# Moving the tiles of a one-core hybrid attention / recurrence layer to 512-byte starts

## The chip, the cores and the metric

The kernel runs on one core of one Trainium2 chip. The metric is the device time of one execution in microseconds (us); lower is better. A profile of one execution is read beside the times. Five kinds of rows appear in it: PE is the matrix engine's matmul stream, PEld its weight loads, DVE the vector engine, ACT the scalar engine, POOL the GpSimd engine; SP only issues transfers.

## The reference

One layer of an encoder for 512 tokens of width 2048, everything in float32. An RMS norm and one projection to 4608 columns give q (8 heads of 128), k and v (2 heads), an attention gate, a recurrent branch's input and its gate. Cut to what matters:

```python
h = rms_norm(x, norm_w)
q, k, v, g_attn, xr, g_lru = split(h @ w_in)            # w_in (2048, 4608)
attn_out = softmax(rope(norm(q)) @ rope(norm(k)).T / sqrt(128)) @ v
xc  = depthwise_conv4(xr) + conv_b
lru = scan(a_fwd, b_fwd) + reversed_scan(a_bwd, b_bwd)  # gates: 128x128 blocks of xc
mixed = concat(rms_norm(attn_out) * silu(g_attn), rms_norm(lru) * silu(g_lru))
return x + mixed @ w_out                                # w_out (2048, 2048)
```

## The kernel before

Each float32 matrix is split into a high and a low part in the matrix engine's rounded float32 format (fp32r), and each product is three matmuls: high by high, high by low, low by high (`mm3`, lines 145 to 147). Nearly all matmuls have a 128 x 128 stationary operand (the one that a weight load brings in ahead of the matmul, 512 bytes of each partition) and a 128 x 512 moving operand (2,048 bytes of each partition, streamed past it). In `nc.tensor.matmul(acc, a, b)`, `a` is stationary and `b` moving.

The order of the matrix engine's work is written out by hand (`manual_schedule`), in these stages, with the times of the profile:

- 0 to 55 us: x is transposed block by block (`xturn`, line 230, 128-column float32 matmuls against the identity `ident`), woven into the first projection (`proj_feat`: weights stationary, x moving).
- 55 to 198 us: a second such projection and k/v (`proj_tok`: x stationary, weights moving) with the recurrence gates (`lru_pair`) between.
- 198 to 262 us: the two q projections (`proj_tok`). Here `wsplit` (lines 204, 205) puts every other pair of weight blocks in a second pool, `wx`.
- 262 to 430 us: attention in 32 steps, with the three gate projections (`proj_feat`) as filling work between. A step makes the scores of 128 queries (`weights`: q slices stationary, `kt` moving), turns an earlier step's probabilities (`turn_weights`, line 575, four 128-column matmuls: the probabilities stationary, `ident` moving), and every fourth step multiplies with v (`values`: v slices stationary, `pt` moving).
- 430 to 498 us: the last gate projection.
- 498 to 654 us: the output projection (`outputs`, line 891) by a scheme with 7 products in place of 8. There are 224 groups of three matmuls: a slice of a combination of the mixed activations is stationary (`mh`, `ml`, eight entries in `mixed`), a combination of `w_out` blocks is moving (`oh`, `ol`). The combination number n goes to slot n % 7 (`operand`): slots 0 to 2 lie in the pool `fin`, slots 3 to 6 in the pool `out`. Entries 0 to 4 of `mixed` lie in `fin` and in the ring `hring`, entries 5 to 7 in `out`.

On-chip memory is laid out by two stacks of pools in each partition. The left stack grows upward: constants (`cp`), raw weights (`wr`), x and split weights (`xw`, later `out`), `rope`, `rot`. The right stack grows downward from byte 229,376: a pad (`end`), the rings of the recurrence and attention results (`hq`), then one after another `lru`, `qkv` with `wx`, `att`, and `fin`. A tile of 4 bytes takes 32. These are the start bytes of tiles that matmuls read, from the program's allocations:

| tile | stack | start byte, example | start modulo 512 |
|---|---|---|---|
| x (`x2`), weights in `xw` (`wh`, `wl`) | left | 37,376; 20,992 | 0 |
| `mh`, `ml`, `oh`, `ol` in `out` | left | 25,088; 88,576 | 0 |
| `ident` | left | 1,152 | 128 |
| weights in `wx` | right | 147,328; 155,520 | 384 |
| raw x blocks, gate operands in `lru` | right | 130,944; 163,712 | 384 |
| `kt`, `v`, rotated q (`ev`) in `qkv` | right | 186,240; 161,664; 176,000 | 384 |
| probabilities turned (`pt`) in `att` | right | 145,280 | 384 |
| probabilities (`k2`) in `att` | right | 126,656 | 192 |
| split q (`b4`) in `att` | right | 110,080 | 0 |
| `mh`, `ml`, `oh`, `ol` in `fin`, `hring` | right | 110,464; 186,240; 196,480 | 384 |

Inside `att` the order from high to low bytes is `pt`, `sm`, `k2`, `mx`, `b4`. `mx` and `sm` hold one number for each query (the row maximum, and the sum of exponentials and its reciprocal), in 6 buffers each: 192 bytes each.

Of the kernel before, what the change touches and what calls it, by code (L numbers as in the profile page):

```python
# [10 lines left out]
F32 = mybir.dt.float32  # L11
# [5 lines left out]
P = 128  # L17
# [38 lines left out]
def hybrid_kernel(  # L56
# [25 lines left out]
    pools, order = {}, {"left": [], "right": []}  # L82

    def opened(name, side):
        pools[name] = tc.alloc_tile_pool(name=name, bufs=1, side=side, reuse_waits="tile")
        order[side].append(name)
        return pools[name]
# [8 lines left out]
    cp = opened("cp", "left")  # L96
    opened("wr", "left")
    opened("xw", "left")
    opened("end", "right").tile([P, 24], F32, tag="end", name="end")
    hring = opened("hq", "right").ring(8 * 2048, name="hring")  # L100
    aring = pools["hq"].ring(8 * 2048, name="aring")
    opened("lru", "right")
# [5 lines left out]
    def nm(s):  # L108
        cnt[0] += 1
        return f"{s}_{cnt[0]}"  # L110
# [7 lines left out]
    def k2(dt=F32, shape=(P, SEQ)):  # L118
        pool, n, _ = work()
        return pools[pool].tile(list(shape), dt, tag="k2", bufs=n, name=nm("k2"))  # L120
# [14 lines left out]
    def mm():  # L135
        return ps.tile([P, SEQ], F32, tag="mm", name=nm("mm"))
# [7 lines left out]
    def mm3(acc, lh, ll, rh, rl, start, stop):  # L144
        nc.tensor.matmul(acc, lh, rh, start=start, stop=False)  # L145
        nc.tensor.matmul(acc, lh, rl, start=False, stop=False)  # L146
        nc.tensor.matmul(acc, ll, rh, start=False, stop=stop)  # L147
# [408 lines left out]
    def weights(q, g, t):  # L556

        qh, ql = q
        tt = slice(t * P, (t + 1) * P)
        sc = mm()  # L560
        mm3(sc, qh[:, tt], ql[:, tt], kth[g], ktl[g], True, True)
        mx = pools["att"].tile([P, 1], F32, tag="mx", bufs=6, name=nm("mx"))
        nc.vector.tensor_reduce(mx, sc, axis=AX.X, op=ALU.max, negate=True)  # L563
        p = k2()
        sm = pools["att"].tile([P, 1], F32, tag="sm", bufs=6, name=nm("sm"))
        nc.scalar.activation(p, sc, AF.Exp, bias=mx, accum_out=sm)
        nc.vector.reciprocal(sm, sm)
        nc.gpsimd.tensor_scalar(p, p, sm, 0.0, op0=ALU.mult, op1=ALU.add)
        return p
# [27 lines left out]
    def attention(rots):  # L597

        qs, ps_, pts = {h: turned(rots[0], h) for h in range(2)}, {}, {}
        yield 13  # L600
        last = NH * NT
        for i in range(last + 3):
            h, t = divmod(i, NT)
            if i < last:
                ps_[i] = weights(qs[h], h // G, t)
                if t == 0 and h + 2 < NH:
                    qs[h + 2] = turned(rots[(h + 2) // G], (h + 2) % G)
            j = i - 3
            if j >= 0 and j % NT == NT - 1:
                values(j // NT, *pts.pop(j // NT))  # L610
            j = i - 2
            if 0 <= j < last:
                h, t = divmod(j, NT)
                if t == 0:
                    pts[h] = [
                        pools["att"].tile([P, NT, SEQ], F32R, tag="pt", bufs=ATT_PT, name=nm("pt"))
                        for _ in range(2)
                    ]
                turn_weights(ps_.pop(j), t, *pts[h])
            yield STEPS  # L620
# [522 lines left out]
```

## Time and profile before

| | |
|---|---|
| median of 3 runs | 661.3 us (661.18 to 662.85) |
| the profiled execution | 660.07 us, of it 658.3 us from the first to the last instruction |
| granted clock of the matrix engine | 0.998 |
| PE busy | 651.0 us, 2971 instructions |
| DVE, ACT, POOL busy | 488.2, 345.6, 92.1 us |
| transfers | 96.17 MB, mean 146 GB/s |

The busy time of PE hides how close its matmuls follow each other: matmuls overlap, and a row's duration (about 390 ns) is longer than the distance from one start to the next. So the distances of starts are what to read: the chain of waits gives, for a run of matmuls with one output bank kind, the start, the length from this start to the next run's, and the count.

### The profile page before, as it was taken

To read this page: it belongs to the slowest core of one execution; us is meant where nothing else is said; L and a number is where in the kernel's file an instruction comes from. 1 tells how busy PE (TensorE), PEld (TensorE's weight loads), DVE (VectorE), ACT (ScalarE), POOL (GpSimd) and SP (SyncE) were. 2 spreads that over 40 slices of the span, in tenths; PEclk is the share of its full clock that TensorE was granted. 3 is DMA by queue.
4 is the path that set the end of the run, shared out by engine and by line. 5 is a ranking of instruction groups with operands and counts; after the bars stand their busy time and mean duration, and the time that the engine had idled before them with its cause. 6 is when DMAs were issued, how large, how long until landed. Compare 5 with 4: busy or idle time off the path is not lost.

```text
span 658.3 us, 8625 instructions
## 1 busy us (share of the span) xinstructions
PE 651.0 (99%) x2971; PEld 534.1 (81%) x2971; DVE 488.2 (74%) x843; ACT 345.6 (53%) x639; POOL 92.1 (14%) x121
## 2 busy tenths in 40 slices
PE   8999999999999999999999999999999999999997
PEld 6888888888888888888888888888888888888875
DVE  5879688977687952855955568439958998698994
ACT  3533898489856515453744446435444564334441
POOL 0000000000022301233443335410000000000000
PEclk9999999999999999999999999999999999999999
DMA  8843252322334321346875768663355766585322
GB/s 291 288 131 93 65 167 65 97 64 67 93 121 135 92 69 32 102 143 154 179 186 138 192 141 199 158 140 95 96 177 199 259 210 237 189 293 181 132 77 96
DMA packets 52731, 96.17 MB, mean 146 GB/s; under 512 B 4184, under 2 KB 14544, under 8 KB 52560
## 3 DMA queue, kind: packets, MB, share of 16 engines
q1 hardware_dynamic: 45648, 75.17, 36.1%
q0 software_dynamic: 6720, 19.93, 13.1%
q10 hardware_dynamic: 320, 0.53, 0.3%
q8 instruction: 23, 0.38, 0.2%
q14 instruction: 20, 0.16, 0.1%
HBM read 91.42 MB, written 20.97 MB: 171 GB/s over the span
## 4 chain that ended last, share of the span: by engine, by line
PE 96%; DVE 1%; DMA 1%; issue 1%; ACT 0%; ACTq 0%; DVEq 0%
PE pj L145 20%; PE pj L147 20%; PE pj L146 20%; PE mm L891 12%; PE pj L891 9%; PE mm L145 3%; PE mm L147 3%; PE mm L146 3%; PE mm L575 2%; PE mm L230 1%; PE pj L287 1%; PE mm L523 1%; DMA nw_st<-in_norm_w_dram 1%; DVE ol L706 0%; DMA rw<-in_w_out_dram 0%
## 5 line engine op out<-in xcount | busy, mean ns | idle before, releaser
L145 PE MATMUL pj<-x,wh 128*128 128x512 f32 x376 | 151.2, 402 | 0.0
L147 PE MATMUL pj<-x,wl 128*128 128x512 f32 x376 | 146.9, 391 | 0.0
L146 PE MATMUL pj<-x,wh 128*128 128x512 f32 x376 | 146.6, 390 | 0.0
L204 ACT CAST wh<-wr 128x512 fp32r<-128x512 f32 x144 | 86.5, 617 | 77.1 <-PE pj L147 28.8
L205 DVE TENSOR_TENSOR wl<-wr,wh 128x512 fp32r<-128x512 f32 x144 | 98.0, 701 | 30.3 <-ACT wh L204 30.3
L147 PEld LDWEIGHTS pj<-x,wl 128*128 128x128 f32 x376 | 70.6, 188 | 15.3
L146 PEld LDWEIGHTS pj<-x,wh 128*128 128x128 f32 x376 | 70.8, 188 | 13.9 <-issue 0.5
L145 PEld LDWEIGHTS pj<-x,wh 128*128 128x128 f32 x376 | 70.7, 188 | 13.8 <-issue 0.5
L145 PE MATMUL pj<-wh,x 128*128 128x512 f32 x192 | 75.6, 394 | 0.0
L147 PE MATMUL pj<-wh,x 128*128 128x512 f32 x192 | 75.2, 392 | 0.0
L146 PE MATMUL pj<-wl,x 128*128 128x512 f32 x192 | 75.1, 391 | 0.0
L705 ACT CAST oh<-rw 128x512 fp32r<-128x512 f32 x94 | 54.8, 618 | 31.6 <-PE mm L891 16.5
L706 DVE TENSOR_TENSOR ol<-rw,oh 128x512 fp32r<-128x512 f32 x94 | 60.5, 685 | 9.7 <-ACT oh L705 8.8
L891 PE MATMUL mm<-ol,mh 128*128 128x512 f32 x128 | 50.3, 393 | 0.5 <-DVE ol L706 0.5
L891 PE MATMUL mm<-oh,mh 128*128 128x512 f32 x128 | 50.2, 392 | 0.0
L891 PE MATMUL mm<-oh,ml 128*128 128x512 f32 x128 | 50.2, 392 | 0.0
L577 ACT CAST pt<-mm 128x512 fp32r<-128x512 f32 x32 | 18.8, 586 | 53.1 <-PE mm L575 53.1
L145 PEld LDWEIGHTS pj<-wh,x 128*128 128x128 f32 x192 | 36.1, 188 | 8.1 <-issue 0.2
L146 PEld LDWEIGHTS pj<-wl,x 128*128 128x128 f32 x192 | 36.1, 188 | 8.0 <-issue 0.2
L147 PEld LDWEIGHTS pj<-wh,x 128*128 128x128 f32 x192 | 36.0, 188 | 7.9
L563 DVE TENSOR_REDUCE mx<-mm 128x1 f32<-128x512 f32 x32 | 22.1, 689 | 24.5 <-PE mm L147 24.0
L891 PE MATMUL pj<-ol,mh 128*128 128x512 f32 x96 | 37.9, 394 | 0.0
(207 smaller groups left out, 1112.0 us busy)
## 6 DMA issues: line engine op xcount, KB each, us to landing
wr<-in_w_in_dram SPq DMA_DIRECT2D x71, 512.0 KB, 3.7
rw<-in_w_out_dram SPq DMA_DIRECT2D x63, 256.0 KB, 3.7
ts<-in_w_out_dram POOLq DMA_DIRECT2D x24, 512.0 KB, 6.7
rw<-ts SPq DMA_DIRECT2D x31, 256.0 KB, 4.6
ts<-ts POOLq DMA_DIRECT2D x8, 512.0 KB, 5.3
xt<-in_x_dram SPq DMA_DIRECT2D x8, 512.0 KB, 8.7
b<-in_x_dram SPq DMA_DIRECT2D x7, 512.0 KB, 7.6
out_dram<-xt POOLq DMA_DIRECT2D x12, 256.0 KB, 3.0
```

The source lines that it names most:

```text
L145: nc.tensor.matmul(acc, lh, rh, start=start, stop=False)
L146: nc.tensor.matmul(acc, lh, rl, start=False, stop=False)
L147: nc.tensor.matmul(acc, ll, rh, start=False, stop=stop)
L204: nc.scalar.copy(hi, raw[:, k, :])
L205: nc.vector.tensor_sub(lo, raw[:, k, :], f(hi))
L230: nc.tensor.transpose(pt[:, t * P : (t + 1) * P], xc[:, t, ks], ident)
L563: nc.vector.tensor_reduce(mx, sc, axis=AX.X, op=ALU.max, negate=True)
L575: nc.tensor.transpose(pt[:, s * P : (s + 1) * P], p[:, s * P : (s + 1) * P], ident)
L577: nc.scalar.copy(pth[:, :, tt], p3)
L705: nc.scalar.copy(hi, src)
L706: nc.vector.tensor_sub(lo, src, f(hi))
L891: nc.tensor.matmul(bank[name, s], lh[:, a, ts_], rh, start=i == 0 and j == 0, stop=i == 7 and j == 2,)
```

## The change

The pad at the top of the right stack grows from 96 to 480 bytes. With the 32 bytes that the stack keeps above it, the first ring's upper end goes from 128 to 512 bytes below byte 229,376, so every pool of the right stack moves down by 384 bytes. In `att`, `mx` and `sm` get 16 buffers each in place of 6, which is 512 bytes each in place of 192; `k2` moves down by 704 bytes in all and `b4` by 1,024. Every tile in the table above then starts at a multiple of 512, but for `ident`, which stays at 1,152. No instruction is added or taken away in the program's text.

```diff
-    opened("end", "right").tile([P, 24], F32, tag="end", name="end")
+    opened("end", "right").tile([P, 120], F32, tag="end", name="end")
...
-        mx = pools["att"].tile([P, 1], F32, tag="mx", bufs=6, name=nm("mx"))
+        mx = pools["att"].tile([P, 1], F32, tag="mx", bufs=16, name=nm("mx"))
...
-        sm = pools["att"].tile([P, 1], F32, tag="sm", bufs=6, name=nm("sm"))
+        sm = pools["att"].tile([P, 1], F32, tag="sm", bufs=16, name=nm("sm"))
```

## The prediction

> **What bounds the kernel.** I read the page's engine totals and its chain first, then the waits of the matrix engine, then the chain in order of time, because busy time can't tell how close the matmuls follow each other.
>
> ```profile
> PE 651.0 (99%) x2971; PEld 534.1 (81%) x2971; DVE 488.2 (74%) x843; ACT 345.6 (53%) x639; POOL 92.1 (14%) x121
> ...
> PE 96%; DVE 1%; DMA 1%; issue 1%; ACT 0%; ACTq 0%; DVEq 0%
> ```
>
> The chain that ended last lies on PE for 96%. The list of PE's own waits is three lines long:
>
> ```profile
> PE mm L179 <- DMA nw_st<-in_norm_w_dram: 1.4, 1, 1.4
> PE mm L924 <- POOL ones L153: 1.1, 1, 1.1
> PE mm L891 <- DVE ol L706: 0.5, 1, 0.5
> ```
>
> 3.0 us in all, two of them at the start. So the time is the number of matmuls times the distance from one start to the next, and only that distance is left to change. Is it the same everywhere? This is the chain at the head of the output stage. Columns: start in us, length up to the next run, what, how many matmuls.
>
> ```profile
> 498.19 2.72 PE mm L891 x12
> 500.91 2.75 PE pj L891 x12
> 503.66 2.80 PE mm L891 x12
> 506.46 2.77 PE pj L891 x12
> 509.24 2.72 PE mm L891 x12
> 511.96 2.79 PE pj L891 x12
> 514.75 2.80 PE mm L891 x12
> 517.55 2.73 PE pj L891 x12
> 520.28 2.75 PE mm L891 x12
> 523.04 2.80 PE pj L891 x12
> 525.84 2.77 PE mm L891 x12
> 528.61 2.98 PE pj L891 x12
> ```
>
> Twelve equal matmuls take 2.72 in one run and 2.80 in another. Lay the placement beside them. Each row is two combinations of w_out by six matmuls; combination n is in slot n % 7, and slots 0 to 2 start at 384 modulo 512, slots 3 to 6 at 0. The rows hold n = 0,1; 2,3; 4,5 and so on. Entries 0 to 4 of `mixed` (rows one to ten) start at 384, entry 5 (the last two rows) at 0.
>
> - Both operands at 384: n = 0,1 (2.72), 8,9 (2.72), 14,15 (2.73).
> - One at 384, one at 0: n = 4,5 (2.80), 10,11 (2.79), 12,13 (2.80), 18,19 (2.80). The last row, n = 22,23 against entry 5, crosses too, with the roles swapped, but a wait is in its 2.98.
> - Half and half: n = 2,3 (2.75), 6,7 (2.77), 16,17 (2.75), 20,21 (2.77).
>
> No row stands against it. Where moving and stationary operands start at the same residue, the distance is 2.72 / 12 = 226.7 ns; where residues differ, 2.80 / 12 = 233 ns. It isn't the right stack that is slow (384 against 384 runs at full pace); it is the mixture. The q stage, where half of the weight blocks are at 384 and x at 0, shows it again. First three rows: 205 to 231 us; the last: one of the three alike groups of the last gate projection, 460 to 495 us, all operands at 0. The last number before the bar's end is the mean ns of one matmul.
>
> ```profile
> L146 PE MATMUL pj<-wl,x 128*128 128x512 f32 x38 | 15.0, 394 | 0.0
> L145 PE MATMUL pj<-wh,x 128*128 128x512 f32 x37 | 14.6, 395 | 0.0
> L147 PE MATMUL pj<-wh,x 128*128 128x512 f32 x37 | 14.6, 395 | 0.0
> ...
> L147 PE MATMUL pj<-x,wl 128*128 128x512 f32 x52 | 20.2, 389 | 0.0
> ```
>
> 394.7 against 389: each is 5.7 ns longer.
>
> **The change, part by part.** It adds no instruction; it moves tiles.
>
> *Output stage.* Of the 224 groups of three matmuls, combinations in slots 3 to 6 against entries 0 to 4 cross, and slots 0 to 2 against entries 5 to 7: 116 groups, 348 matmuls, counted through the 112 combinations in their order, each used by two groups. By the rows above a crossing matmul costs (2.80 - 2.72) / 12, from the means of the four undisturbed and three matched rows 6.2 ns: 348 x 6.2 = 2.2 us. The other end is the whole stage, its first and last of 672 matmuls:
>
> ```profile
> 498.03 0.39 PE L891 MATMUL mm<-oh,mh 128*128 128x512 f32 x1
> ...
> 653.70 0.39 PE L891 MATMUL mm<-oh,ml 128*128 128x512 f32 x1
> ```
>
> 671 distances in 155.67 us; 671 x 226.7 = 152.1, so 3.5 us are over, of which 0.7 are waits (0.5 in the list above, 0.2 in the 2.98 row). That leaves 2.8. I take 2.5, between them: the total holds every matmul, but also pauses too short to be listed.
>
> *Attention.* One step in order of time (start us, duration us); left out are the three score matmuls and two of the gate projection:
>
> ```profile
> 345.05 0.39 PE L147 MATMUL pj<-x,wl 128*128 128x512 f32 x1
> ...
> 345.97 0.60 PE L575 MATMUL mm<-ident,k 128*128 128x128 f32 x4
> 346.33 0.48 PE L145 MATMUL pj<-x,wh 128*128 128x512 f32 x1
> ...
> 347.11 0.39 PE L145 MATMUL pj<-x,wh 128*128 128x512 f32 x1
> ```
>
> The score matmuls stream `kt` (384) past q slices (0). From 345.05 to 345.97 four matmuls take 0.92 us against 4 x 0.2267 = 0.907; from 345.97 to 347.11 four transposes and three matmuls take 1.14 against 4 x 0.109 (the 0.60 row: three distances and a last one of 0.27) + 3 x 0.2267 = 1.116. So 13 ns a step before the transposes and 24 behind them, with 10 ns of rounding in each. The change aligns the first part. The second stays: `ident` remains at 128, and a 128-against-0 crossing is there today and after. I count 32 x 16 = 0.5 us (between 13 and the three crossing matmuls at 6.2 = 19) and 0.1 for the borders between `values` (384 against 384, no loss now) and its neighbours: 0.6. If the part behind the transposes vanished as well, about 50 blocks of transposes x 16 to 24 ns would be 0.8 to 1.2 us more; if nothing, 0.
>
> *q stage, 198.8 to 258.4 us* (first and last matmul that streams a block from `wx`). In it lie 243 projection matmuls, half with moving blocks at 384. The group rows say 5.7 ns each for both halves, so a crossing also delays its neighbours. One matmul behind four transposes in the group rows' window has a longer duration that is no longer distance (the 0.48 row above against 0.39): 0.09 us, 0.8 ns a matmul over 112. 243 x 4.9 = 1.2 us.
>
> *Everything else on PE.* The input transposes, the gates of the recurrence and k's transposes enter and leave residue 384 about 39 times: 39 x 6.2 = 0.2 us.
>
> *More buffers for `mx` and `sm`.* Their groups:
>
> ```profile
> L563 DVE TENSOR_REDUCE mx<-mm 128x1 f32<-128x512 f32 x32 | 22.1, 689 | 24.5 <-PE mm L147 24.0
> ```
>
> The maximum waits for the scores, 24.0 of 24.5 us, not for a free buffer; a step is some 5 us long (262 to 430 us by 32) and six buffers last 30 us. Nothing gained, nothing lost.
>
> *What is late next.* DVE and ACT prepare the operands, and their pace doesn't rise:
>
> ```profile
> 500.00:560.00 60.00, 60.00 (x261) 48.59 (x260) 54.49 (x87) 33.77 (x56) 1.23 (x2) 1.00 0.72 246
> ```
>
> (Columns after the window: length, PE, PEld, DVE, ACT, POOL, granted clock, share and GB/s of transfers.) DVE is busy 54.5 of 60 us; 1.6% faster matmuls leave 59 us, still enough on the mean. But once DVE already ended PE's run:
>
> ```profile
> 611.84 0.60 ACT ev L853
> ...
> 627.12 0.61 DVE ol L706
> ```
>
> From 611.84, when a first product is finished, 15.9 us of work on ACT and DVE lead to the operand that PE needed. In that time PE issues some 66 matmuls, half of them crossing, and would be there 66 x 0.5 x 6.2 = 0.2 us sooner, only to wait. That 0.2 goes back. Elsewhere PE has no wait on operands, so the matmul time saved is time saved.
>
> *Other engines.* Their operands move too. The split's subtraction, from 62 to 178 us (all at 0) and from 205 to 258 us (half in `wx`):
>
> ```profile
> L205 DVE TENSOR_TENSOR wl<-wr,wh 128x512 fp32r<-128x512 f32 x34 | 21.9, 683 | 6.7 <-ACT wh L204 6.7
> ...
> L205 DVE TENSOR_TENSOR wl<-wr,wh 128x512 fp32r<-128x512 f32 x17 | 11.4, 686 | 7.6 <-ACT wh L204 7.6
> ```
>
> 683 and 686 ns: indifferent within 3 ns. Zero.
>
> *The sum:* 2.5 + 1.2 + 0.6 + 0.2 - 0.2 = 4.3 us. The profiled execution is 660.07 us, 658.3 of it span, 1.2 below the median of 661.3. Off the median: 657.0 (a profiled span near 654.0).
>
> [...]
>
> **Rivals.** (1) *The residue is not the cause.* The stationary and moving streams don't touch, and what I read as crossing is something else that goes with slots, such as which buffers were written just before. Then 661.3. For it: the runs correlate only. Against it: four combinations of one stage sort without exception, and three stages with all operands at one residue agree at 226.7 or 389. [...]
>
> (2) *The output stage is held by DVE.* If the operand supply, at 54.5 of 60 us, is what paces PE over longer stretches than the one at 611 to 627, the stage's 2.3 us net come back as waits: 657.0 + 2.3 = 659.3. Against it: PE waited for `ol` once, 0.5 us.
>
> (3) *The transposes' exits vanish as well*, if 128 against 0 is harmless once the tile transposed is at 0: 0.8 to 1.2 more, 656.0. Against it: the pair that leaves the transposes (`ident` at 128, then a weight at 0) is the same after.
>
> (4) *Slower:* with every tile at one residue, DVE and ACT accesses now meet PE's, and DVE operations lengthen. The place is the output stage. DVE's 54.5 us in 60 leave room for 8% with today's PE. It decides from about +10%; at +13% (690 to 780 ns) 61.6 us of DVE work for each 60 add 1.6 us there, 4.2 over the stage's 156 us, and the 2.3 us that the stage was to gain are lost as well, while the 2.0 elsewhere stay: 661.3 + 4.2 - 2.0 = 663.5. Against it: 683 and 686 ns, where the all-at-0 stage is the quicker.
>
> **How the numbers follow.** My forecast 0.72, rival 1 0.08, rival 2 0.09, rival 3 0.08, rival 4 0.03. A difference of 0.3% (2.0 us) is about what can be told from no change, so faster means below 659.3. Forecast and rival 3 are faster; rival 2 falls on the bound, half to each side: faster 0.85, same 0.12, slower 0.03. The forecast's own range is 655.9 to 658.1: sums of 3.2 (output 2.2, q 0.9, attention 0.4, others 0.1, back 0.4) to 5.4 (output 2.8, q 1.3, attention 0.6 and 0.5 of exits, others 0.2). To take in rival 3 with its 1.2 and rival 2, 655.6 to 659.3.
>
> **What would show it.** In the profile after, the output stage's chain has 2.72 in all twelve rows, and the q stage's groups have a mean near 389 to 390. In an attention step the four matmuls up to the transposes take 0.91; the part behind them keeps its 24 ns. The wait of PE on `ol` near 625 us grows from 0.5 to about 0.7. DVE's mean for line 205 stays at 683 to 686 and its instruction count at 843. I am wrong if rows of 2.80 remain in the output stage, if PE's list of waits gains more than 1 us, or if the exits lose their 24 ns.

## The result, and the profile after

The changed kernel takes 657.4 us, median of 6 runs (656.62 to 658.75), against 661.58 us for the kernel before in the same comparison (6 runs, 661.17 to 662.85). The ratio is 0.9941, 95% interval 0.9924 to 0.9958. Predicted was 657.0.

The profiled execution took 657.92 us, its span is 656.1 (before 660.07 and 658.3); a span near 654.0 had been forecast. Its engine totals and PE's own waits:

```profile
PE 648.4 (99%) x2971; PEld 535.1 (82%) x2971; DVE 489.3 (75%) x843; ACT 345.9 (53%) x639; POOL 92.2 (14%) x121
```

```profile
PE mm L179 <- DMA nw_st<-in_norm_w_dram: 1.2, 1, 1.2
PE mm L924 <- POOL ones L153: 1.1, 1, 1.1
PE mm L891 <- DVE ol L706: 0.8, 1, 0.8
PE pj L891 <- DVE ol L706: 0.4, 1, 0.4
```

The same instructions; the waits on `ol` have become two, 1.2 us in place of 0.5. Now the distances. The run that took 2.80 us before (the third of the twelve, combinations 4 and 5) no longer lies on the chain, so here are the first matmul of it and of the run behind it, in order of time:

```profile
503.02 0.39 PE L891 MATMUL mm<-oh,mh 128*128 128x512 f32 x1
...
505.74 0.39 PE L891 MATMUL pj<-oh,mh 128*128 128x512 f32 x1
```

2.72 us for twelve. By the starts no row of 2.80 is left among the twelve: eleven take 2.72 us, and the twelfth, which now holds a wait, 3.47. From 531 us the chain shows 2.72 for every run, halves of 1.36 included (before, the same rows had 2.74 to 2.79 and 1.36 to 1.40):

```profile
531.13 5.44 PE mm L891 x24
536.57 5.44 PE pj L891 x24
542.01 2.72 PE mm L891 x12
544.73 1.36 PE pj L891 x6
546.09 2.72 PE mm L891 x12
```

And the groups of the q stage, 205 to 231 us, 389 to 392 ns in place of 394 to 395:

```profile
L145 PE MATMUL pj<-wh,x 128*128 128x512 f32 x38 | 14.9, 392 | 0.0
L147 PE MATMUL pj<-wh,x 128*128 128x512 f32 x38 | 14.8, 390 | 0.0
L146 PE MATMUL pj<-wl,x 128*128 128x512 f32 x38 | 14.8, 389 | 0.0
```

An attention step, in order of time, with the same matmuls as in the prediction:

```profile
344.53 0.39 PE L147 MATMUL pj<-x,wl 128*128 128x512 f32 x1
...
345.44 0.60 PE L575 MATMUL mm<-ident,k 128*128 128x128 f32 x4
345.80 0.48 PE L145 MATMUL pj<-x,wh 128*128 128x512 f32 x1
...
346.58 0.40 PE L145 MATMUL pj<-x,wh 128*128 128x512 f32 x1
```

The four matmuls up to the transposes take 0.91 us, the seven from there 1.14, both as forecast.

To account for the whole span I took from both traces the distance of each matmul's start to the next, less 226.7 ns (109 for a transpose), and added these up by stage. Anything over 20 ns more counts as a pause and stands by itself. "Nominal" below means without this excess.

| us over nominal | before | after | predicted gain | measured gain |
|---|---|---|---|---|
| q stage, 180 to 262 us | 1.36 | 0.12 | 1.2 | 1.24 |
| attention, 262 to 430 us | 1.72 | 1.75 | 0.6 | 0.0 |
| output, from 500 us | 2.56 | 0.08 | 2.5 | 2.48 |
| the other stages | 0.56 | 0.39 | 0.2 | 0.17 |
| pauses in the output stage | 1.00 | 1.78 | -0.2 | -0.8 |
| pauses up to 60 us | 0.66 | 1.44 | 0 | -0.8 |
| other pauses | 0.99 | 1.00 | 0 | 0 |

The sum is 2.3 us, the spans differ by 2.2. The medians differ by 4.2. The row on pauses up to 60 us explains a part of that: the start differs from execution to execution (last section), the profiled execution of before had a good one and is quicker than each of its six timed runs, and the after one is not. With equal starts the spans would differ by 3.0 us, or 0.5%, inside the interval. The remaining 1.2 us between 3.0 and 4.2 are no saving that a trace shows. Three of the changed kernel's six times lie at 656.6 to 656.9 and three at 657.9 to 658.8; the six of before all lie at 661.17 or more, though in later comparisons some of its runs took 660.1 to 660.3. So the six runs of before probably had fewer good starts; only profiled executions can show a start.

### The profile page after: what moved, and what is told of

It reads as the page before. It is cut to its first block, busy times and chain, and to the rows that moved or that the text cites. A ratio compares the mean times of both kernels' runs of the same rounds, so it can differ in the third digit from the quotient of the medians.

```text
span 656.1 us, 8620 instructions
## 1 busy us (share of the span) xinstructions
PE 648.4 (99%) x2971; PEld 535.1 (82%) x2971; DVE 489.3 (75%) x843; ACT 345.9 (53%) x639; POOL 92.2 (14%) x121
## 4 chain that ended last, share of the span: by engine, by line
PE 91%; DVE 5%; issue 1%; DMA 1%; ACT 1%; DVEq 0%; ACTq 0%
PE pj L145 20%; PE pj L147 20%; PE pj L146 20%; PE mm L891 9%; PE pj L891 7%; PE mm L147 3%; PE mm L145 3%; PE mm L146 3%; DVE ol L706 2%; PE mm L575 2%; PE mm L230 1%; PE pj L287 1%; PE mm L523 1%; DMA nw_st<-in_norm_w_dram 1%; ACT mh L687 0%
```

## The experiments

**Equal residues, or multiples of 512?** The changed kernel has the identity at 128 and all else at 0. Two variants put everything at one residue: at 0, and at 384, where nothing starts at a multiple of 512.

`e1_ident0`, on the changed kernel:

```diff
+    const([P, 96], "pad0")
     ident = const([P, P], "ident")
+    const([P, 32], "pad1")
```

> The changed kernel, with 384 bytes of pad ahead of the identity and 128 behind it, so that the identity too starts at a multiple of 512 and no operand of any large matmul differs in residue. If what the transposes leave behind in the changed kernel (the matmuls after each block of transposes are 5 to 10 ns late, about 50 ns for each of the 32 attention steps, 2.0 us in all over the attention and input stages) is a crossing of 128 against 0, it vanishes: about 655.4 us, 0.991 of before, and the second and third matmul behind a block of transposes are 227 ns from start to start. If it comes from the change of matmul kind itself, nothing changes: 657.4 us, 0.994 of before, and the 230 to 235 ns behind the transposes stay.

Measured: 657.97 us, ratio to before 0.9945 (0.9931 to 0.996). No difference in time from the changed kernel. Of the changed kernel's 2.34 us over nominal 1.99 are left, and the matmuls just behind the transposes are still late: over the 32 attention steps the second and third take 233 and 234 ns on the mean (changed kernel 234 and 232). So most of the tail does not hang on the identity's residue: 39 of the 51 ns a step stay. That it comes from the change of matmul kind is my reading; no run shows that by itself. The attention stage alone goes from 1.71 to 1.36 us (280 to 430 us).

`e2_all384`, on the kernel before:

```diff
+    const([P, 64], "pad0")
     ident = const([P, P], "ident")
+    const([P, 32], "pad1")
...
-        mx = ... bufs=6          # sm likewise
+        mx = ... bufs=16
```

> The kernel before, with the left stack and the identity moved up so that everything on the left starts at 384 modulo 512, as the right stack already does, and with 16 buffers for the two small tiles; nothing starts at a multiple of 512. If equal residues are what counts, this is as quick as the kernel with everything at multiples of 512 including the identity (about 655.4 us if the transposes' tail goes, 657.4 if not), and all twelve runs at the head of the output stage take 2.72 us. If starts at multiples of 512 are what counts, every run takes 2.80 us or more: 2688 matmuls by 6 ns, about 16 us more than the best, over 670 us.

Measured: 658.34 us, 0.9957 (0.9945 to 0.9969). The chain of the output stage (two lines were added above, so line 891 is 893 here):

```profile
536.80 5.44 PE pj L893 x24
542.24 2.72 PE mm L893 x12
544.96 1.36 PE pj L893 x6
546.32 2.72 PE mm L893 x12
```

All at 384 runs like all at 0: 1.93 us over nominal in the whole kernel, 0.04 in the output stage. Multiples of 512 count for nothing by themselves (2.72 us for twelve at 384 as at 0); the two operands' difference does (2.80 before). That also rules out rival 1, that something else goes with the slots: slots and order are as before, and only the left stack's residue has moved, but for the 16 buffers, which alone leave the output stage at 2.59 us (`e4_bufs_only`, next).

**Which half of the change does it?** `e3_pad_only` is the pad without the buffers, `e4_bufs_only` the buffers without the pad.

```diff
e3:  -    opened("end", "right").tile([P, 24], ...)
     +    opened("end", "right").tile([P, 120], ...)
e4:  -        mx = ... bufs=6          # sm likewise
     +        mx = ... bufs=16
```

> The change's pad alone, small attention tiles with 6 buffers as before: in attention, keys (0) then cross the queries (128), and the probabilities start at 320; the rest is as in the changed kernel. My theory: output stage and q stage as after, 2.72 us in all runs and a mean of 389 to 390 ns in the q stage; the score matmuls lose 10 to 18 ns a step, 0.3 to 0.6 us in all: 657.4 to 658.2 us. If the buffers do part of the work by being more, attention loses more than that.

> The change's 16 buffers alone, the pad as before: the queries then start at 384 like the keys, and everything on the right is at 384. My theory: output and q stage as before (2.72 and 2.80 us by turns, 394 to 395 ns); the score matmuls gain 10 to 18 ns a step: 661.0 to 661.4 us, no difference that can be told from before. If the change's gain came from more buffers, it would be near 657.4.

Measured: the pad alone 659.46 us, 0.997 (0.9958 to 0.9981); the buffers alone 661.03 us, 0.9994 (0.9984 to 1.0005). The pad does the output and q stages: 0.06 and 0.12 us over nominal, as after. But with it alone keys and queries differ by 128 and probabilities and identity by 192, and attention is worse than before: 2.77 us over nominal between 280 and 430 us against 1.67. The score matmuls' groups there, in `e3_pad_only`:

```profile
L145 PE MATMUL mm<-kt,b 128*128 128x512 f32 x31 | 12.5, 404 | 0.0
L147 PE MATMUL mm<-kt,b 128*128 128x512 f32 x31 | 12.4, 399 | 0.0
L146 PE MATMUL mm<-kt,b 128*128 128x512 f32 x31 | 12.2, 395 | 0.0
```

Against the changed kernel (1.71) I had expected a loss of 0.3 to 0.6 us here; it is 1.1, and by what I wrote beforehand a larger loss would speak for the number of buffers. The distances speak against it. PE has no pause in this stretch, and the loss sits on the matmuls whose operands differ: the three score matmuls are 241, 233 and 236 ns from start to start on the mean (227, 227 and 230 in the changed kernel), and the one ahead of them, whose next weights are the queries, 232 in place of 227. That is 32 ns a step, 1.0 us of the 1.1. So what I had wrong is the price of a crossing, up to 14 ns here in place of 6, and the buffers matter as space, 320 bytes more for each of the two kinds. No run gives the space without the number.

**What is the grain?** In four variants the right stack, with 16 buffers, starts at 256, 128, 64 and 32 modulo 512, the left at 0. Each ran once, for its profile, so only the distances are read here. Against the changed kernel the only edit is the pad:

```diff
-    opened("end", "right").tile([P, 24], ...)
+    opened("end", "right").tile([P, 56], ...)      # 256; 88, 104, 112 for 128, 64, 32
```

> Right stack at 256 modulo 512 (left at 0, 16 buffers for the small tiles). If any difference of residue costs the same, the crossing runs at the head of the output stage take 2.80 us (233 ns a matmul), and the q stage's mean is 394 to 395 ns. If the price goes with the distance, 256, the largest that there is modulo 512, costs most (over 2.85 us).

> Right stack at 128 modulo 512. Any difference alike: crossing runs 2.80 us. Price by distance: the same 2.80 as at 384, which is 128 the other way round. The identity is at 128 too here, so the raw x blocks and the probabilities equal it.

> Right stack at 64 modulo 512. Any difference alike: crossing runs 2.80 us. Price by distance: between 2.72 and 2.80, about 2.76. If only multiples of 64 matter as a unit (one block of 64 bytes being the grain), 64 would be as harmless as 0: 2.72.

> Right stack at 32 modulo 512, the smallest step of the placement. Any difference alike: crossing runs 2.80 us. Price by distance: about 2.74. If what counts is the offset inside a 64-byte block, this one costs and the one at 64 does not.

The q stage's groups, first of `e5_right256`, then of `e5_right32`:

```profile
L146 PE MATMUL pj<-wl,x 128*128 128x512 f32 x39 | 15.2, 389 | 0.0
L145 PE MATMUL pj<-wh,x 128*128 128x512 f32 x38 | 14.9, 392 | 0.0
L147 PE MATMUL pj<-wh,x 128*128 128x512 f32 x38 | 14.8, 390 | 0.0
```

```profile
L147 PE MATMUL pj<-wh,x 128*128 128x512 f32 x38 | 14.9, 393 | 0.0
L145 PE MATMUL pj<-wh,x 128*128 128x512 f32 x37 | 14.8, 399 | 0.0
L146 PE MATMUL pj<-wl,x 128*128 128x512 f32 x37 | 14.5, 391 | 0.0
```

| right stack modulo 512 | output stage, us over nominal | mean distance of a matmul whose moving operand and next weights are on different stacks, ns |
|---|---|---|
| 384 (buffers alone) | 2.59 | 232.7 |
| 256 | 0.06 | 226.8 |
| 128 | 2.56 | 232.7 |
| 64 | 2.61 | 232.3 |
| 32 | 2.84 | 233.4 |

None of my ideas holds whole. The price doesn't grow with the distance; 64 is not harmless; and not every difference costs: 256 costs nothing at all, while 32, 64, 128 and 384 cost 5.6 to 6.7 ns a matmul in this stage. Of the differences tried, those that are multiples of 256 bytes are free and no others. Timed, the 256 variant confirms it:

> Right stack at 256 modulo 512, left at 0, timed (one look had shown the q stage at 389 to 392 ns). If the grain is 256 bytes, it is as quick as the changed kernel: 657.9 us, 0.9945 of before, within 0.15%. If multiples of 512 gave something that the matmul distances don't show, it is slower than that, 659 us.

Measured: 657.72 us, 0.9943 (0.9931 to 0.9956), the changed kernel's time. It needs 128 bytes more of pad, not 384.

**Where did 0.6 us of the output stage go?** PE's pauses on `ol` grew in every variant with equal residues (1.0 us before, 1.8 in the changed kernel and in five variants). The changed kernel's chain up to the first of its two waits runs through DVE:

```profile
521.31 2.49 DVE ol L706 x4
523.80 0.61 DVE t L677
...
527.58 0.69 DVE ol L706
528.32 2.81 PE pj L891 x11
```

I tried to take work from DVE: sixteen operations of the output stage that touch no matmul bank go to POOL, which is busy for 1.2 of the 60 us from 500 to 560.

```diff
-                v.tensor_add(b11, b11, tmp["a", s])
+                nc.gpsimd.tensor_add(b11, b11, tmp["a", s])
...              # likewise b01 -= b, b10 += c, and the last gates' product
```

> The changed kernel, with 16 additions and products of the output stage that touch no matmul bank (the running sums b11, b01 and b10 in done, the last gates' products) on POOL in place of DVE. If the two waits of PE on an operand of DVE in the changed kernel (0.4 us listed at 527 us and 0.8 at 625 us, 1.8 us over the nominal distances) are DVE's own pace, both shrink, and the stage gains up to 1.2 us: about 656.8 us, 0.993 of before. If the operand was late for its transfer, or POOL's slower operations (1.3 us each in place of 0.7) hold DVE's later ones, the waits stay or grow: 657.8 us or more.

Measured: 662.06 us, 1.0005 (0.9996 to 1.0014), about 0.6% slower than the changed kernel. The matmul distances stay good (2.72 us for twelve from 631 us on), but the output stage's pauses go from 1.8 to 5.1 us. In order of time, POOL's two products and DVE's four operations beside them:

```profile
519.03 3.42 POOL L634 TENSOR_TENSOR av<-av,ev 128x512 f32<-128x512 f32 x2 [6.36 <-DVE ev L633]
...
519.54 4.67 DVE L706 TENSOR_TENSOR ol<-rw,oh 128x512 fp32r<-128x512 f32 x4
```

In the changed kernel four such DVE operations in a row take 2.49 us, here 4.67, of which POOL works beside them for 2.9. The groups from 500 to 530 us, this kernel and then the changed one:

```profile
L706 DVE TENSOR_TENSOR ol<-rw,oh 128x512 fp32r<-128x512 f32 x20 | 16.2, 871 | 0.5 <-ACT oh L705 0.5
```

```profile
L706 DVE TENSOR_TENSOR ol<-rw,oh 128x512 fp32r<-128x512 f32 x23 | 14.3, 684 | 0.0
```

In the stretch with POOL's products the mean goes from 684 to 871 ns. What lengthens these operations, no run here shows. The attempt failed, but with a slower DVE the two largest pauses are in the changed kernel's two places and longer (1.1 us at 527 us and 1.3 at 627, against 0.6 and 1.0), and new ones stand beside them. So DVE's pace is what the waits hang on.

The same edits with the identity at a multiple of 512 and more warm-up matmuls:

```diff
-WARM, WARM2 = 13, 6
+WARM, WARM2 = 17, 6
```

> Identity at a multiple of 512, the 16 operations on POOL, and 17 warm-up matmuls in place of 13. Up to about 10 us the first matmuls run from start to start at 427 ns in some runs and at 227 in others; if that comes from the idle time before the first transposes, four more warm-up matmuls (0.85 us at that pace) keep the engine active and save 0.5 to 1.5 us; with the operations on POOL: 655.5 to 656.5 us, 0.991 to 0.992 of before. If the slow distances fall by chance, or end at a time that the warm-up doesn't move, it is as the kernel with the operations on POOL.

Measured: 660.43 us, 0.9989 (0.998 to 0.9998). That misses the 655.5 to 656.5 us. The operations on POOL cost it what they cost the other: 5.1 us of pauses in the output stage. The warm-up is left open. The profiled start is a good one, but so are some with 13 warm-up matmuls. The times hint at an effect: the median is 1.6 us below `e6_less_dve`, of which the identity explains some 0.4, and eight of 11 runs are within 0.8 us of the quickest, against two of 11 there. No run changes the warm-up alone, so it isn't shown.

**A deeper ring.** If DVE's mean pace suffices and only its bursts don't, operands have to be made earlier. On `e1_ident0`:

```diff
-    NW, WF = 7, 3
+    NW, WF = 8, 3
...
-        tag, n = ("rw", 10) ...
+        tag, n = ("rw", 8) ...
```

> The kernel with the identity at a multiple of 512, operations all on DVE as before, and 8 operand slots of the output stage in place of 7 (raw w_out blocks have 8 buffers in place of 10, to make room). An operand may then be ready one combination (1.36 us of matmuls) earlier. If the waits of PE at 527 and 625 us (1.8 us over nominal in all) are DVE falling behind in bursts, a deeper ring covers them: up to 1.8 us less, 656.2 us, 0.992 of before. If the two raw buffers that it costs make the loads late instead, the waits stay or grow: 658 us or more.

Measured: 656.47 us, 0.9927 (0.9914 to 0.9941), the quickest here, and its profiled execution has the shortest span, 653.0 us. PE's waits in the output stage are gone; its list has two lines:

```profile
PE mm L181 <- DMA nw_st<-in_norm_w_dram: 1.3, 1, 1.3
PE mm L926 <- POOL ones L155: 1.1, 1, 1.1
```

The head of the output stage has all its runs at 2.72 and one at 2.73:

```profile
518.20 2.72 PE mm L893 x12
520.92 2.72 PE pj L893 x12
523.64 2.72 PE mm L893 x12
526.36 2.73 PE pj L893 x12
529.08 5.44 PE mm L893 x24
```

while DVE is as busy as ever, 54.8 of 60 us:

```profile
500.00:560.00 60.00, 60.00 (x267) 49.65 (x266) 54.79 (x87) 34.00 (x56) 1.23 (x2) 1.00 0.75 254
```

So the 0.8 us that the output stage gave back were bursts of DVE work that a ring of seven no longer covered at the faster pace, not DVE's share of the time.

## Why the prediction was right, point by point

The time came out 0.4 us above the forecast, and the mechanism is the one forecast: operands at one residue, start distances of 226.7 ns. That it came so close is partly luck. The traces show a gain of 3.1 us without the row on the start, against 4.3 forecast and just below 3.2, the lowest sum in the forecast's range; and the profiled span missed its 654.0 by 2.1. Two terms were wrong, attention by 0.6 us and the give-back by 0.6, and the medians hide it because the two sets of six runs seem to differ in their starts. Point by point:

- *Output stage* (2.5 forecast, 2.48 measured) and *q stage* (1.2, 1.24): right, as rows at 2.72 us and groups at 389 to 392 ns show. The others (0.2) came to 0.17.
- *Attention* (0.6 forecast, 0.0 measured): the step "the second stays" failed. The first part moved as it should: the score matmuls' mean durations between 280 and 430 us were 395, 387, 394 ns and are now

```profile
L147 PE MATMUL mm<-kt,b 128*128 128x512 f32 x31 | 12.1, 391 | 0.0
L145 PE MATMUL mm<-kt,b 128*128 128x512 f32 x31 | 12.1, 389 | 0.0
L146 PE MATMUL mm<-kt,b 128*128 128x512 f32 x31 | 12.1, 389 | 0.0
```

  Their three distances together were 11 ns a step over nominal and are 4, all of it before the transposes: 0.24 us gained over the 32 steps, half of the 0.5 forecast. The `values` matmuls gained another 0.15, against 0.1 forecast, though their operands agreed before as after: behind the crossing scores their first four were late. But the twelve matmuls behind the transposes together went from 36 to 51 ns over nominal: 0.5 us lost. My 24 ns were read off the first three, and those did stay (20 on the mean before, 22 after). The delay fades over about twelve, and the other nine went from 16 to 29. I held it fixed because its last pair, identity and weight, didn't change. What did change is probabilities against identity, from 64 bytes apart to 128. In the variants where these two agree modulo 256 (buffers alone, right at 128, both all-equal ones) attention stands at 1.26 to 1.36 us over nominal, where they are 128 apart at 1.70 to 1.73. That the pair counts is shown. With 64 apart in `e5_right64` the twelve are 40 ns late, near the 36 of before; why 64 apart is cheaper here than 128 is open.
- *Rival 3*, that the exits from the transposes vanish in the changed kernel: no, they grew. `e1_ident0`, where the identity crosses with nothing, still keeps 39 of the 51 ns.
- *What is late next*: mis-sized. Forecast 0.2 us more for one wait; measured 0.8 more, at 527 us and at 625. I had counted the wait that I saw growing, and had not looked for operands that were just in time before. The 2.98 row, at 528.61 us, was such a wait in small: a weight load waited 0.4 us there for `ol` from DVE. Rival 2 was thus partly true: not 2.3 us, but 0.8.
- *Other engines*: right. DVE's count is 843 and line 205's median 684 ns (683 before); rival 4 did not come. Its room of 8% is the one with the faster PE (59 us against 54.5); with PE as it was it is 10%.
- *Rival 1*, that the residue is not the cause: out by `e2_all384`, with 0.04 us over nominal in the output stage against 2.56 before. With weights whose start agrees with the running matmul's operand modulo 256 the distance is 226.7 to 226.8 ns, with others about 6 ns more in the output stage. What in the chip makes the difference, no run here shows.

## What to carry to other kernels

Where PE is never idle, look at the distance of matmul starts, not at busy time, and compare it between runs of equal matmuls: 2.72 against 2.80 us for twelve was the whole finding. For matmuls like these, give the tiles that supply stationary and moving operands starts that agree modulo 256 bytes, on both sides of the memory (in the output stage here 226.7 to 226.8 ns from start to start, 232 to 233 at the other differences tried), and check what small tiles between them do to that; here the bytes of two kinds of 4-byte tiles decided 1.1 us of attention. When PE gets quicker, operands that were just in time become waits (here 1.0 us of pauses in the output stage became 1.8): look one ring slot ahead before the gain is booked.

## What the runs showed of the hardware

- In the output stage a matmul with 512 moving columns of rounded float32 and a fresh weight load is followed by the next after 226.7 to 226.8 ns when its moving operand and the next weights start equal (the changed kernel) or 256 bytes apart modulo 512 (`e5_right256`). At differences of 32, 64, 128 (`e5_right32`, `e5_right64`, `e5_right128`) and 384 (`e4_bufs_only`) it is 232 to 233 ns on the mean. The price is not one number: the score matmuls of `e3_pad_only`, at a difference of 128, take 233 to 241. At a border the pair that counts is the running matmul's moving operand and the following one's stationary: the last matmul of a gate projection, with both its operands at 0, takes 232 ns on the mean when the next one's weights are at 384 (`e4_bufs_only`), and 227 when they are at 0 (before).
- The delay carries over to matmuls that don't cross. Before, the first four of a `values` block, with all operands at 384, take 236, 228, 232 and 231 ns behind the crossing scores, in seven of the eight blocks alike within 1 ns; in the changed kernel 226 to 227.
- In attention a block of four 128-column float32 transposes leaves the next matmuls late, 39 ns in all over about twelve with all residues equal (`e1_ident0`), 51 with probabilities and identity 128 apart (the changed kernel).
- The first projection's matmuls start slow for a varying time. In order of time, four of them before, and four in `e4_bufs_only`:

```profile
7.00 1.20 PE L287 MATMUL pj<-x,wh 128*128 128x512 f32 x4
```

```profile
7.96 2.06 PE L287 MATMUL pj<-x,wh 128*128 128x512 f32 x4
```

  In the second, two of the distances are 427 ns, nearly twice 227, though the granted clock reads 1.00 there. The first matmul of line 267 (269 where two lines were added), behind the first projection, starts at 53.4 to 53.8 us in five profiled executions and at 54.4 to 56.2 in the nine others. The same program with the right stack at 256 has both kinds, with spans of 655.0 and 656.9 us. The warm-up matmuls just ahead of the first projection's (line 924, 256 columns) differ in the same way: 109 ns from start to start before, from 6.06 us on, and 213 in the changed kernel, from 6.41 to 7.47 us. What ends the slow stretch, no run here shows.
